# Hybrid attention block on one core: scores made once in two-bank tiles, probabilities scaled and transposed by TensorE, sinks' blocks first, output projection beside blocks

## Chip, cores and metric

One Trainium2 chip; the kernel runs on one of its cores. The metric is the device time of the core in microseconds, the median of the runs shown. All inputs are 32-bit floats.

## The reference

Two layers over 1024 tokens of width 1024. Layer 0 is a mixer of two attentions, layer 1 an mLSTM; each is followed by a SwiGLU FFN with 2816 hidden columns. The change is in layer 0's mixer:

```python
qa, kc, vc, ks, vs, kw, vw, g, qb, kb, vb = split(h @ w_in)         # 2072 columns; 8 query heads on 2 key heads, 64 wide
# attention a, per block of 128 queries, for three sets of keys:
#   compressed (63 keys), selected (16 of 16 key blocks: all earlier ones), window (512)
p = masked_softmax(q @ k.T * scale, mask);  o_i = p @ v
o_a = gate_0 * o_c + gate_1 * o_s + gate_2 * o_w                     # gates = sigmoid(g + gate_bias)
# attention b, per block: window of 128, and a sink in the softmax
mx = max(logits.max(-1), sink);  e = exp(logits - mx)
o_b = (e / (e.sum(-1) + exp(sink - mx))) @ v
h = h + concat(o_a, o_b) @ w_out
```

## The kernel before

All products are made in the type F32R from split operands: a value x is hi (its rounding, made by a copy) and lo = x - hi. `product` (line 138) makes one 128x512 output from k chunks with three matmuls each (hi x hi, hi x lo, lo x hi): 24 for the input projection, 12 for the output projection here. `split_w` (line 122) makes the parts of weights; `load_w` brings them with one DMA.

Queries are written to DRAM (`qs`) and read back per block with head dimension on partitions. K and V stay in SBUF pages. `page(tag)` takes pages from five pools with a fixed count each (`PAGES`); PSUM tiles come from `acc` and `tmp_ps` and, for the statistics, from a third tag "ts".

A block is 128 queries of one key head g: four heads r, so 512 columns. There are 16 blocks of attention a ("NSA blocks", kind 0) and 16 of attention b ("sinks' blocks", kind 1). `block` (line 523) is a generator of four steps:

1. three DMAs bring the queries as qa and qb (line 531), GpSimd clears the rest of qb (line 533).
2. `scores_stats` (line 488): for each head r the scores with queries on partitions (two matmuls per stretch of keys, lines 496 and 498), the row's minimum of negated masked scores (line 507; line 503 without mask) and the exponent with its sum (line 509). Only minimum and sum are kept.
3. the correction (minimum, log of sum, log of gate, per query and key set) is joined, split, transposed by TensorE (line 612) and written into qb's lower rows (line 613).
4. for each chunk of 128 keys the scores are made again with keys on partitions: matmuls of qa (line 639), qb with the correction (line 640) and, on masked chunks, of the mask (line 642); the exponent (line 644) is then the final probability, split by `parts` (lines 103, 105, 108), and goes into two value products (lines 646 and 647). At the end `po` is copied (line 649), its two halves are joined and split by GpSimd (lines 101, 653, 654) and written to DRAM (`os`).

`blocks` (line 665) keeps four blocks in flight, each one step behind the next. `mixer_ab` (line 676) runs the first part of the input projection alone (compressed keys, first half of qa, selected and window keys and values, gates). Then it draws one dense product per block: the 16 of the second part (rest of qa, attention b's columns) beside the 16 NSA blocks, then the output projection of attention a (`ab_out(0)`, line 694) beside the sinks' blocks. The output projection of attention b, with the next norm, follows at the end.

The order in which each engine runs its instructions is set when the program is built: a planner takes what it expects to be ready, earlier written work first, so that dense products fill gaps of the blocks and the other way round. At run time each engine keeps that order.

## Time and profile before

| what | value |
|---|---|
| median of 3 runs | 2661.21 us (2660.42 to 2661.75) |
| profiled execution | 2661.99 us, its span 2660.3 us |
| mean granted TensorE clock | 0.987 |
| TensorE busy | 2578.3 us (97%) |
| VectorE, ScalarE, GpSimd busy | 1344.4, 725.5, 480.4 us |

Busy times are of one profiled execution. A matmul's row shows its whole passage (about 0.39 us for 512 columns) while the next one starts much earlier, so counts in a stretch say more than durations. Clock 1.00 is 2.4 GHz, the lower level 1.2 GHz; a number between is a mean over a stretch.

### The profile page before, as it was taken

The page shows a single profiled execution, that of the slowest core. Times are in us where ns is not written, and L with a number is a line of the kernel's source. Part 1 is how long each engine was busy: PE and PEld are TensorE (multiplying, and loading weights), DVE is VectorE, ACT ScalarE, POOL GpSimd, SP SyncE. Part 2 cuts the span into 40 slices and gives each one's busy share as a digit, 9 for nine tenths or more (in the row PEclk, how much of TensorE's full clock was granted, in tenths as well). Part 3 has the DMA queues.
Part 4 walks back from the last instruction along what each step waited for, and adds up shares of the span by engine and source line. Part 5 has one row for each costly group of instructions (what it writes and reads, how often), then busy time and mean ns, then how long its engine had stood idle before and what let it go on. Part 6 is the DMA issues. An engine that isn't in the chain of part 4 may idle for free.

```text
span 2660.3 us, 29873 instructions
## 1 busy us (share of the span) xinstructions
PE 2578.3 (97%) x11365; PEld 2053.8 (77%) x11365; DVE 1344.4 (51%) x2675; ACT 725.5 (27%) x1685; POOL 480.4 (18%) x542
## 2 busy tenths in 40 slices
PE   8999999988999999999999999999999999999998
PEld 6877777665778888888887777788788888888886
DVE  4368878988643333333336554545533333333335
ACT  4247768744210000000002343332210000000013
POOL 3322132154301010101012111112110101010102
PEclk9999999989999999999999999999999999999999
DMA  6222131343311111111113111112111111111112
GB/s 192 89 71 72 51 97 28 112 108 83 102 48 48 48 48 48 48 48 48 48 48 112 52 41 40 36 56 95 48 32 55 41 50 46 48 48 48 56 48 79
DMA packets 178899, 167.36 MB, mean 63 GB/s; under 512 B 15220, under 2 KB 156740, under 8 KB 178756
## 3 DMA queue, kind: packets, MB, share of 16 engines
q1 hardware_dynamic: 178756, 165.46, 20.1%
q8 instruction: 89, 1.46, 0.2%
q14 instruction: 54, 0.44, 0.0%
HBM read 136.02 MB, written 29.38 MB: 62 GB/s over the span
## 4 chain that ended last, share of the span: by engine, by line
PE 86%; DVE 7%; ACT 2%; issue 2%; POOL 1%; DMA 1%; SPq 0%; DVEq 0%; ACTq 0%; POOLq 0%
PE acc L144 12%; PE acc L145 12%; PE acc L143 12%; PE pg L145 6%; PE pu L144 6%; PE pu L143 6%; PE pu L145 6%; PE pg L144 6%; PE pg L143 6%; PE po L647 2%; PE po L646 2%; DVE lo L108 1%; PE sps L498 1%; PE sps L496 1%; PE st L639 1%
## 5 line engine op out<-in xcount | busy, mean ns | idle before, releaser
L103 ACT CAST whl<-ws 128x1024 fp32r<-128x1024 f32 (+2 forms) x112 | 95.0, 848 | 870.1 <-PE acc L145 435.2
L144 PE MATMUL acc<-lo,whl 128*128 128x512 f32 x800 | 316.2, 395 | 0.0
L143 PE MATMUL acc<-hi,whl 128*128 128x512 f32 x800 | 315.2, 394 | 0.0
L145 PE MATMUL acc<-hi,whl 128*128 128x512 f32 x800 | 314.1, 393 | 0.0
L101 POOL TENSOR_SCALAR whl<-ws 128x1024 fp32r<-128x1024 f32 (+2 forms) x132 | 116.0, 879 | 1011.7 <-PE acc L145 472.0
L143 PE MATMUL pu<-xh,whl 128*128 128x512 f32 x704 | 279.7, 397 | 0.0
L145 PE MATMUL pg<-xh,whl 128*128 128x512 f32 x704 | 278.2, 395 | 0.6 <-DVE whl L108 0.6
L143 PE MATMUL pg<-xh,whl 128*128 128x512 f32 x704 | 278.1, 395 | 0.0
L145 PE MATMUL pu<-xh,whl 128*128 128x512 f32 x704 | 278.1, 395 | 0.0
L144 PE MATMUL pu<-xl,whl 128*128 128x512 f32 x704 | 278.1, 395 | 0.0
L144 PE MATMUL pg<-xl,whl 128*128 128x512 f32 x704 | 278.0, 395 | 0.0
L143 PE MATMUL acc<-xh,whl 128*128 128x512 f32 x640 | 262.8, 411 | 0.1
L144 PE MATMUL acc<-xl,whl 128*128 128x512 f32 x640 | 259.2, 405 | 2.5 <-DVE xl L200 2.3
L145 PE MATMUL acc<-xh,whl 128*128 128x512 f32 x640 | 257.4, 403 | 0.5 <-DVE whl L108 0.5
L108 DVE TENSOR_TENSOR whl<-ws,whl 128x1024 fp32r<-128x1024 f32 (+2 forms) x222 | 220.1, 991 | 39.5 <-ACT whl L103 23.0
L238 DVE TENSOR_TENSOR u<-pu,rb 128x512 f32<-128x512 f32 x88 | 60.8, 691 | 353.9 <-PE pu L145 353.9
L788 DVE TENSOR_TENSOR h<-h,acc 128x512 f32<-128x512 f32 x176 | 120.7, 686 | 231.8 <-PE acc L145 231.7
L143 PEld LDWEIGHTS acc<-hi,whl 128*128 128x128 f32 x800 | 150.3, 188 | 36.3 <-POOL hi L101 0.3
L145 PEld LDWEIGHTS acc<-hi,whl 128*128 128x128 f32 x800 | 150.2, 188 | 35.4
L144 PEld LDWEIGHTS acc<-lo,whl 128*128 128x128 f32 x800 | 150.1, 188 | 34.8 <-DVE lo L108 0.2
L766 ACT ACTIVATE g<-g 128x512 f32<-128x512 f32 x88 | 55.5, 631 | 437.6 <-DVE g L238 436.8
L101 POOL TENSOR_SCALAR hi<-u 128x512 fp32r<-128x512 f32 x88 | 82.8, 941 | 486.4 <-DVE u L769 486.4
(316 smaller groups left out, 4563.1 us busy)
## 6 DMA issues: line engine op xcount, KB each, us to landing
ws<-in_ffn_w_gate SPq DMA_DIRECT2D x22, 1024.0 KB
ws<-in_ffn_w_up SPq DMA_DIRECT2D x22, 1024.0 KB
ws<-in_ffn_w_down SPq DMA_DIRECT2D x40, 512.0 KB
spill<-h SPq DMA_DIRECT2D x32, 256.0 KB
qa<-qs SPq DMA_DIRECT2D x64, 128.0 KB
os<-o SPq DMA_DIRECT2D x64, 128.0 KB
h<-spill SPq DMA_DIRECT2D x32, 256.0 KB
oh<-os SPq DMA_DIRECT2D x32, 256.0 KB
```

Source lines behind the costliest of these rows:

```text
L101: nc.gpsimd.tensor_scalar(out, in_, 1.0, 0.0, op0=OP.mult, op1=OP.add)
L103: nc.scalar.copy(out, in_)
L108: self.nc.vector.tensor_tensor(out, in_, hi.bitcast(F32), op=OP.subtract)
L143: nc.tensor.matmul(ps, w[:, 0, k], xh, start=(start and k == 0), stop=False)
L144: nc.tensor.matmul(ps, w[:, 0, k], xl, start=False, stop=False)
L145: nc.tensor.matmul(ps, w[:, 1, k], xh, start=False, stop=(stop and k == n - 1))
L238: nc.vector.tensor_tensor(out, ps, self.rb(hf), op=OP.mult)
L496: nc.tensor.matmul(p[:, at:at + n], qa[:, r * P:(r + 1) * P], ka, start=True, stop=False, skip_group_check=True)
L646: nc.tensor.matmul(po, vt, eh, start=(i == 0), stop=False)
L647: nc.tensor.matmul(po, vt, el, start=False, stop=(i == len(todo) - 1))
L766: silu = nc.scalar.activation(g, g, AF.Silu)
L788: nc.vector.tensor_add(h, h, ps)
```

## The change

Scores are made once. `scores` makes them with queries on partitions in a tile S of two PSUM banks (two of them), 1024 columns wide, so that one row of any key set fits; a stretch of keys that crosses the border between the banks is cut. One masked minimum and one exponent per head follow, the exponent written to SBUF (page "x"; "w" for compressed keys and sinks' blocks). `weights` makes one factor per row (from sum and gate, or sum and sink) and GpSimd scales the four rows. `values` transposes 128x128 pieces of the scaled probabilities with TensorE, four into one bank T, ScalarE copies hi, VectorE subtracts lo, and two value products follow per chunk. `blocks` writes, for each unit (a block's key set): weights of the unit before, scores of this unit, values of the unit before. Queries are loaded two blocks ahead with four DMAs.

K pages hold hi and lo in their two halves (one page instead of two). The gate is kept as 1 + exp(-z). During the mixer `acc` and `tmp_ps` have two tiles each. A pair of hi and lo in tag "x" is one page of double width; the count of "x" pages goes from 32 to 16.

Attention b's columns come first in the input projection (`first`, 12 products), then its blocks run beside the rest (`second`, 20 products and the gates, 22 steps drawn over 15 blocks). The NSA blocks run beside the output projection of attention b (`out1`, 16 products, two per block in the first eight) and beside half of that of attention a (`out0`, 8 products, one per block from n = 4 on). The other half (8 products) follows with the norm of both halves. h is kept in "k" pages and layer 0's hid in "h" pages. The core of the diff:

```diff
-PAGES = {"x": 32, "h": 16, "k": 20, "w": 10, "q": 8}
+PAGES = {"x": 16, "h": 16, "k": 20, "w": 10, "q": 8}
...
+    def pair(self, tag, name):
+        if tag == "x":
+            t = self.page("x", name, F32R, w=2 * H5)
+            return t[:, :H5], t[:, H5:]
+        return self.page(tag, name, F32R), self.page(tag, name, F32R)
     def acc(self, name="acc"):
+        if self.attn:
+            return self.ps.tile([P, H5], F32, name=name, tag="pa", bufs=2)
         return self.ps.tile([P, H5], F32, name=name, tag="acc", bufs=3)
     def tmp_ps(self, name="tp"):
+        if self.attn:
+            return self.ps.tile([P, H5], F32, name=name, tag="T", bufs=2)
         return self.ps.tile([P, H5], F32, name=name, tag="tp", bufs=3)
...
-        xh = self.page("x", f"xh", F32R)
-        xl = self.page("x", f"xl", F32R)
+        xh, xl = self.pair("x", "xh")
...
+            k = self.page("h" if br < 2 else "k", "K", F32R)
+            s, o = slice(64 * g, 64 * g + 64), slice(64 - 64 * g, 128 - 64 * g)
+            self.hi_copy(k[s], kf[s], "act")
+            self.lo_sub(k[o], kf[s], k[s])
+            self.K[br, g, hf] = k
...
-                nc.vector.tensor_scalar(z, z, self.gbias, None, op0=OP.add)
-                self.log_sigmoid(z, z)
...
+                nc.vector.tensor_scalar(z, z, self.gbias, -1.0, op0=OP.add, op1=OP.mult)
+                nc.vector.tensor_scalar(z, z, 88.0, None, op0=OP.min)
+                nc.scalar.activation(z, z, AF.Exp)
...
+        first = [(KB, [k_tile(2), v_tile(2)]), (QB, [q_tile(1, 0), q_tile(1, 1)]),
+                 (QB + 256, [q_tile(1, 2), q_tile(1, 3)])]
+        second = [(KC, [c_tile(0), c_tile(1)]), (KS, [k_tile(0), v_tile(0)]), (KW, [k_tile(1), v_tile(1)]),
+                  (QA, [q_tile(0, 0), q_tile(0, 1)]), (QA + 256, [q_tile(0, 2), q_tile(0, 3)])]
         first, second = [[part(*x) for x in xs] for xs in (first, second)]
+        return chain(*first), chain(*second, g_part())
...
+                k = self.at.tile([P, 64], F32R, name=f"kc{g}")
+                nc.vector.memset(k.bitcast(F32), 0.0)
+                nc.scalar.copy(k[0:64, :nb], po[:64, :nb])
+                nc.vector.tensor_tensor(k[64:128, :nb], po[:64, :nb], k[0:64, :nb].bitcast(F32), op=OP.subtract)
+                self.Kc[g] = k
...
-    def scores_stats(self, qa, qb, parts, width, mask, nm, ls):
...
+    def load_q(self, kind, g, n):
+        nc = self.nc
+        qa, qb = self.pair("q", "qa")
+        for i, t in enumerate((qa, qb)):
+            src = self.qs[kind, i, 256 * g:256 * g + 256, n * P:(n + 1) * P].rearrange("(r d) q -> d r q", d=64)
+            for k in range(2):
+                self.last_q = nc.sync.dma_start(t[64 * k:64 * k + 64].bitcast(F32).rearrange("d (r q) -> d r q", r=4), src)
+        return qa, qb
...
+    def units(self, kind, g, n):
+        def vals(br, first):
+            return [self.V[br, g, j // 4][:, (j % 4) * P:(j % 4 + 1) * P] for j in range(first, n + 1)]
+        mks, mkw = (m.rearrange("p a b -> p (a b)") for m in (self.mks, self.mkw))
         if kind == 0:
+            first = max(0, n - 4)
+            w, ww = (n + 1) * P, (n + 1 - first) * P
+            return [(0, [(self.Kc[g], 0)], 64, self.mkc[:, 56 - 8 * n:120 - 8 * n], [self.Vc[g]]),
+                    (1, self.key_parts(0, g, 0, n), w, mks[:, 1024 - w:], vals(0, 0)),
+                    (2, self.key_parts(1, g, first, n), ww, mkw if n >= 4 else mks[:, 1024 - ww:], vals(1, first))]
+        first = max(0, n - 1)
+        w = (n + 1 - first) * P
+        return [(3, self.key_parts(2, g, first, n), w, self.mkw[:, 0:5:4] if n else self.mkw[:, 4], vals(2, first))]
...
+    def scores(self, q, unit, g):
+        nc = self.nc
+        br, parts, w, mask, _ = unit
+        qa, qb = q
+        st = self.sm.tile([P, 4, 4], F32, name="st", bufs=6)
+        es = []
+        if br == 0:
+            ec = self.page("w", "ec", w=256).rearrange("p (r k) -> p r k", r=4)
+        for r in range(4):
+            h = slice(r * P, (r + 1) * P)
+            p = self.ps.tile([P, 2 * H5], F32, name="S", bufs=2)
+            cuts = []
+            for k, at in parts:
+                n = k.shape[1]
+                m = min(n, H5 - at % H5)
+                cuts.append((k[:, :m], at))
+                if m < n:
+                    cuts.append((k[:, m:], at + m))
+            for k, at in cuts:
+                n = k.shape[1]
+                for i, qq in enumerate((qa, qb)):
+                    nc.tensor.matmul(p[:, at:at + n], qq[:, h], k, start=i == 0, stop=i == 1, skip_group_check=True)
+            s = p[:, :w]
+            sv = s.rearrange("p (a b) -> p a b", a=mask.shape[1]) if len(mask.shape) == 3 else s
+            nm, l = st[:, 0, r:r + 1], st[:, 1, r:r + 1]
+            nc.vector.tensor_tensor_reduce(sv, sv, mask, -1.0, 1e20, OP.add, OP.min, nm)
+            if br == 3:
+                nc.vector.tensor_tensor(nm, nm, self.sink[:, 4 * g + r:4 * g + r + 1], op=OP.min)
+            if br == 0:
+                e = ec[:, r]
+            elif br == 3:
+                if r % 2 == 0:
+                    e2 = self.page("w", "e3")
+                e = e2[:, r % 2 * 256:r % 2 * 256 + w]
             else:
+                e = self.page("x", "e", w=w)
+            nc.scalar.activation(e, s, AF.Exp, bias=nm, scale=-1.0, accum_out=l)
+            es.append(e)
+        return st, es
...
+    def weights(self, unit, g, n, st, es):
+        nc = self.nc
+        br = unit[0]
+        nm, l, t, f = (st[:, i] for i in range(4))
+        if br == 3:
+            nc.vector.tensor_tensor(t, nm, self.sink[:, 4 * g:4 * g + 4], op=OP.subtract)
+            nc.scalar.activation(t, t, AF.Exp)
+            nc.vector.tensor_tensor(t, t, l, op=OP.add)
         else:
+            ig = self.ig[:, n, g * 12:(g + 1) * 12].rearrange("p (r b) -> p b r", b=3)[:, br]
+            nc.vector.scalar_tensor_tensor(t, l, 0.5, ig, op0=OP.max, op1=OP.mult)
+        nc.vector.reciprocal(f, t)
+        for r in range(4):
+            nc.gpsimd.tensor_scalar(es[r], es[r], f[:, r:r + 1], 0.0, op0=OP.mult, op1=OP.add)
+    def values(self, unit, es, po, first, last):
+        nc = self.nc
+        br, _, w, _, vals = unit
+        for j, v in enumerate(vals):
+            tp = self.tmp_ps("T")
+            n = min(P, w)
+            for r in range(4):
+                nc.tensor.transpose(tp[:n, r * P:(r + 1) * P], es[r][:, j * P:j * P + n], self.ident)
+            eh, el = self.pair("k", "eh")
+            if br == 0:
+                for t in (eh, el):
+                    nc.gpsimd.memset(t[64:128].bitcast(F32), 0.0)
+            nc.scalar.copy(eh[:n], tp[:n])
+            nc.vector.tensor_tensor(el[:n], tp[:n], eh[:n].bitcast(F32), op=OP.subtract)
+            nc.tensor.matmul(po, v, eh, start=first and j == 0, stop=False)
+            nc.tensor.matmul(po, v, el, start=False, stop=last and j == len(vals) - 1)
...
-    def block(self, kind, g, n, big):
...
+        work = []
+        for b in todo:
+            us = self.units(*b)
+            work += [(b, u, i == 0, i == len(us) - 1) for i, u in enumerate(us)]
+        qs = {}
+        def ahead(i):
+            if i < len(todo):
+                qs[todo[i]] = self.load_q(*todo[i])
+        ahead(0)
+        ahead(1)
+        done = None
+        for i in range(len(work) + 1):
+            cur = work[i] if i < len(work) else None
+            prev = done
+            if prev:
+                self.weights(prev[0][1], prev[0][0][1], prev[0][0][2], *prev[1])
+            if cur:
+                (kind, g, n), unit, first, last = cur
+                if first:
+                    ahead(todo.index(cur[0]) + 2)
+                done = (cur, self.scores(qs[cur[0]], unit, g))
+            if prev:
+                b, unit, first, last = prev[0]
+                if first:
+                    po = self.acc("po")
+                self.values(unit, prev[1][1], po, first, last)
+                if last:
+                    self.outputs(*b, po)
+                yield b, last
...
+            self.h = [[None] * NC for _ in range(2)]
+            n = 0
+            for i, _ in enumerate(self.blocks([(1, g, n, ) for n in range(8) for g in range(2)])):
+                want = (i + 1) * 22 // 15
+                while n < want and next(second, self) is not self:
+                    n += 1
+            for _ in second:
                 pass
+            out1 = self.ab_out(1, (0, 1))
+            out0 = self.ab_out(0, (0,))
+            for b, last in self.blocks([(0, g, n) for n in range(8) for g in range(2)]):
+                if last and next(out1, self) is self and b[2] >= 4:
+                    next(out0, None)
+                elif last:
+                    next(out1, None)
+            for _ in chain(out1, out0):
+                pass
+        self.attn = False
         self.norm_begin()
+        for c, _ in enumerate(self.ab_out(0, (1,))):
+            for hf in range(2):
+                self.norm_chunk(self.h[hf][c], hf, c, "nf", 0)
...
+    def ab_out(self, part, hfs):
         nc = self.nc
         w_out = self.a["ab_w_out"][0]
+        xs = {hf: [] for hf in hfs}
+        for hf in hfs:
             for c in range(4 * part, 4 * part + 4):
+                t = self.page("x", "oh", F32R, w=2 * H5)
+                with self.behind():
+                    nc.sync.dma_start(t.bitcast(F32).rearrange("p (i t) -> p i t", i=2),
+                                      self.os[:, c * P:(c + 1) * P, hf * H5:(hf + 1) * H5].rearrange("i p t -> p i t"))
+                xs[hf].append((t[:, :H5], t[:, H5:]))
         for c2 in range(4):
             ws = self.load_w(w_out[H5 * part:H5 * part + H5, c2 * 256:(c2 + 1) * 256], 4)
+            for i in range(2):
+                c = c2 * 2 + i
+                w = self.split_w(ws[i])
+                for hf in hfs:
+                    if part:
+                        h = self.h[hf][c] = self.page("k", "h")
+                        with self.behind():
+                            nc.sync.dma_start(h, self.spill[c][:, hf * H5:(hf + 1) * H5])
                     h = self.h[hf][c]
                     ps = self.acc()
                     self.product(ps, w, xs[hf])
                     nc.vector.tensor_add(h, h, ps)
                     yield
+    def behind(self):
+        return self.tc.issue_after(self.last_q.ins)
...
-                        hid[m + i, hf] = self.parts(u, "k", "pool")
+                        hid[m + i, hf] = self.parts(u, "k" if last else "h", "pool")
```

## Rows read from the trace of the kernel before

**Rows 1.** The page's first part: busy time of an engine, its share of the span, its instructions.
```profile
PE 2578.3 (97%) x11365; PEld 2053.8 (77%) x11365; DVE 1344.4 (51%) x2675; ACT 725.5 (27%) x1685; POOL 480.4 (18%) x542
```

**Rows 2.** Busy time by stretch: from:to and length in us, busy us and instructions of TensorE, its weight loads, VectorE, ScalarE and GpSimd, granted clock, DMA share, GB/s.
```profile
20.00:50.00 30.00, 25.15 (x138) 18.36 (x139) 20.08 (x39) 13.65 (x31) 10.86 (x11) 1.00 0.62 194
50.00:100.00 50.00, 50.00 (x294) 41.32 (x294) 10.61 (x19) 7.50 (x16) 11.03 (x8) 0.90 0.32 107
100.00:175.00 75.00, 71.86 (x326) 56.06 (x325) 36.17 (x76) 21.29 (x58) 25.49 (x21) 0.95 0.24 72
175.00:500.00 325.00, 307.85 (x1398) 243.60 (x1397) 276.35 (x849) 244.31 (x731) 77.41 (x74) 0.97 0.23 70
500.00:650.00 150.00, 128.16 (x543) 96.06 (x542) 131.46 (x340) 82.00 (x232) 70.22 (x74) 0.93 0.36 96
650.00:723.00 73.00, 65.44 (x257) 49.05 (x258) 47.58 (x70) 17.53 (x29) 26.40 (x28) 0.95 0.35 110
800.00:1460.00 660.00, 660.00 (x2837) 531.50 (x2835) 256.35 (x344) 66.31 (x95) 84.01 (x105) 1.00 0.17 54
```

**Rows 3.** The chain of work that ended last, 655 to 725 us: start, duration, what.
```profile
662.31 0.59 ACT oc L649
...
667.57 3.92 DMA os<-o
671.50 4.91 DMA oh<-os
...
717.32 0.51 PE pg L145
```

**Rows 4.** Waits, 175 to 735 us: engine and line, for whom it waited, us in total, times, longest.
```profile
ACT sps L509 <- DVE st L507: 30.8, 47, 3.3
...
PE po L647 <- DVE lo L108: 15.8, 20, 1.5
```

**Rows 5.** TensorE in order of time (start, duration, what), in five places: score matmuls of 256, of 64 and of 384 columns, matmuls of 512 columns where the clock had fallen (with the row of busy time by stretch for it), and the transposes of h (with theirs).
```profile
343.77 0.28 PE L496 MATMUL sps<-ka,qa 128*128 128x256 f32 x1
343.89 0.28 PE L498 MATMUL sps<-kb,qb 88*128 88x256 f32 x1
...
362.12 0.28 PE L496 MATMUL sps<-kac,qa 128*128 128x64 f32 x1
362.23 0.28 PE L498 MATMUL sps<-kbc,qb 88*128 88x64 f32 x1
...
368.91 0.34 PE L496 MATMUL sps<-ka,qa 128*128 128x384 f32 x1
369.09 0.34 PE L498 MATMUL sps<-kb,qb 88*128 88x384 f32 x1
...
585.86 0.63 PE L143 MATMUL acc<-oh,whl 128*128 128x512 f32 x1
586.29 0.63 PE L144 MATMUL acc<-oh,whl 128*128 128x512 f32 x1
...
2575.77 7.15 PE L804 MATMUL tp<-ident,h 128*128 128x128 f32 x64
...
580.00:590.00 10.00, 9.79 (x34) 8.04 (x35) 7.75 (x23) 3.65 (x14) 3.75 (x4) 0.66 0.32 80
...
2576.00:2582.60 6.60, 6.60 (x63) 6.60 (x62) 1.88 (x2) 6.14 (x13) 1.06 (x1) 1.00 0.01 2
```

**Rows 6.** Groups of TensorE instructions, 40 to 735 us: line, operation, tiles, count, busy us and mean ns of one, idle before.
```profile
L496 PE MATMUL sps<-ka,qa 128*128 128x256 f32 (+3 forms) x264 | 85.0, 330 | 1.8 <-ACT sps L509 1.0 <-DVE h L719 0.4 <-DMA qa<-qs 0.4
...
L647 PE MATMUL po<-lo,vt 128*128 128x512 f32 x162 | 72.3, 446 | 8.9 <-DVE lo L108 8.8
...
L639 PE MATMUL st<-qa,ka 128*128 128x512 f32 x162 | 68.0, 419 | 2.7 <-ACT e L644 1.7 <-DVE qf L240 0.5 <-DVE qb L613 0.4
...
L642 PE MATMUL st<-identr,mk 128*128 128x512 f32 x70 | 28.6, 409 | 0.0
...
L464 PE MATMUL tp<-kvs,cw 128*64 128x63 f32 x128 | 15.6, 296 | 0.0
L496 PE MATMUL sps<-kac,qa 128*128 128x64 f32 x64 | 14.3, 240 | 0.9 <-ACT sps L509 0.9
```

**Rows 7.** VectorE in order of time (start, duration, what), then groups (as above) of VectorE and ScalarE, 40 to 735 us, and of GpSimd, whole span.
```profile
474.21 0.69 DVE L503 TENSOR_REDUCE st<-sps 128x1 f32<-128x512 f32 x1
474.81 0.69 DVE L507 CUSTOM_DVE_ANT_0 sps<-sps,mk 128x512 f32<-128x512 f32 x1
475.42 0.14 DVE L507 DVE_READ_ACCUMULATOR2_ANT st<- 128x1 f32 x1
475.42 0.69 DVE L108 TENSOR_TENSOR lo<-e,hi 128x512 fp32r<-128x512 f32 x1
...
L105 DVE CAST hi<-e 128x512 fp32r<-128x512 f32 x108 | 48.1, 445 | 0.7 <-ACT e L644 0.2
...
L509 ACT ACTIVATE sps<-sps,st 128x512 f32<-128x512 f32 x72 | 47.7, 662 | 14.4 <-DVE st L507 7.4 <-DVE st L503 6.5
...
L101 POOL TENSOR_SCALAR whl<-ws 128x1024 fp32r<-128x1024 f32 x76 | 81.4, 1071 | 615.0 <-PE acc L145 258.0 <-PE pu L145 201.0 <-issue 138.3
L199 POOL TENSOR_SCALAR xh<-h,vec 128x512 fp32r<-128x512 f32 x64 | 57.0, 894 | 136.7 <-DVE h L739 41.1 <-DVE h L719 28.8 <-DVE h L788 28.4
...
L101 POOL TENSOR_SCALAR whl<-ws 128x512 fp32r<-128x512 f32 x52 | 32.9, 633 | 373.8 <-PE acc L145 203.8 <-issue 168.9 <-POOL xh L199 0.5
```

More of the change, by code (lines that the diff above doesn't have):

```diff
@@ L648, in block, with outputs @@
+    def outputs(self, kind, g, n, po):
+        nc = self.nc
         c = self.page("w", "oc")
@@ L660, in blocks @@
     def blocks(self, todo):
-        live = [None] * 4
-        for b in list(todo) + [None] * 3:
-            live = [self.block(*b) if b else None] + live[:3]
-            for i in ORDER:
-                if live[i]:
-                    next(live[i], None)
-            yield
+        work = []
[27 more added lines that the diff above has]
+                yield b, last
     def mixer_ab(self):
```

242 lines of the change are left out of this document (25 added, 217 removed).

## The prediction

> **What bounds the kernel now.** I read the page's engine totals first: TensorE is busy 97% of the span and no other engine more than 51% [rows 1]. That makes it the suspect everywhere, but a modelled busy time is no rate, so I read the busy time by stretch next, beside the granted clock. In the first FFN (800 to 1460 us) TensorE is busy all the time at clock 1.00 and issues 2837 matmuls in 660 us, 0.233 us each [rows 2]: this is what a 128x512 matmul costs when nothing is late. The change touches nothing there. It touches 20 to 717 us, where layer 0's mixer runs; the first FFN product starts at 717.3 us [rows 3].
>
> Inside it the stretches differ. I multiply busy share by clock for a net share. 175 to 500 us (NSA blocks beside 24-matmul input products): 307.85/325 = 0.95, times 0.97, 0.92. 500 to 650 us (sinks' blocks beside 12-matmul output products): 128.16/150 = 0.85, times 0.93, 0.79. There VectorE is busy 131 of 150 us [rows 2]: TensorE waits for small VectorE steps. So the stage is TensorE's, with VectorE close behind (0.85 of 175 to 500 us), and it gets worse where the dense products beside the blocks get thin. PE waits named by the profile are short: 20 waits for the lo part before a value product, 15.8 us in all [rows 4].
>
> A second measure counts work. Priced at 0.233 us per 512-column matmul, at the issue distances of [rows 5] for smaller ones (0.12 us for 256 columns, 0.175 for 384, 0.11 for 64 and 128) and 0.11 us per transpose, the stage holds: input products 16x2x24 x 0.233 = 179; output products 8x2x2x12 x 0.233 = 90; transposed scores (162 + 16)x2 matmuls and 70 + 16 mask matmuls (the 16s are the compressed chunk, one per NSA block), 442 x 0.233 = 103; value products 356 x 0.233 = 83; statistics' scores, 264+64 pairs, 97 by their shapes in the code (72, 88, 40 and 128 pairs of 512, 256, 384 and at most 128 columns); compression, gates and transposes some 40 [rows 6]. Sum 592 us in 697: 0.85. Over 20 to 717 us busy times clock is about 0.88, so waits too short to show as idle take another 0.03.
>
> **The change part by part.** *Scores once.* Removed from TensorE: 356 transposed score matmuls (83 us), 86 mask matmuls (20 us), 32 transposes of the correction, one per block (3.5 us): 106.5 us. Added: four transposes for each of 178 key chunks, 712 x 0.11 = 78 us. The before's own 64 transposes of h in one go took 7.15 us at clock 1.00 [rows 5], 0.11 us each, and they are the same operation on the same shape. Rows of 640 columns and more are cut at the bank border: for n = 5, 6, 7 one more cut per row and query part, 48 small matmuls x 0.11 = 5 us. Net 23 us less on TensorE.
>
> *VectorE, ScalarE, GpSimd.* VectorE loses 108 copies of hi parts [rows 7], the write of the correction and some dozen small operations per block; it keeps one masked minimum per row (now up to 1024 columns) and one lo part per chunk. Consecutive 512-column operations start 0.60 us apart although each is shown as 0.69, and reading the accumulator costs no start [rows 7]: so 0.07 + 0.00104 us per column. For the NSA blocks: 71680 score columns in 192 rows, 88 us; 148 lo parts x 0.6 = 89; some 20 of small ones; 30 of dense work beside them: 227 us. ScalarE: exponents at 0.66 us for 512 columns [rows 7], copies at 0.59 [rows 3]: about 200 us. GpSimd gets new work, the scaling of probabilities: 1.05 us for 1024 columns in the nearest row (weights, 1071 ns), 0.89 for 512 by the dearer one (xh with a scale per partition) [rows 7]; so between 0.2 us a row + 0.00085 us a column (from that row and its 512-column sister, 633 ns) and 0.00175 us a column, 99 to 125 us for the NSA rows. I take the lower, because that row has the larger tile; with the unchanged outputs it stays well under 285 us. Against TensorE's sum below, none of the three is the bound. The scaling is cheap as work and dear as a wait: the four rows of a unit (up to 4 x 1.05 us) must all be done before the first transpose of that unit; behind a waiting transpose on TensorE stand the unit's value products and the dense and score matmuls that the planner put after them. What hides it is the next unit's scoring, which the new loop writes between the two; without that cover 48 units x 2 to 4 us would show, 100 to 190 us.
>
> *Sinks' blocks first.* They now run beside 20 input products of 24 matmuls instead of 16 output products of 12. Start and first part: products begin at 20 to 21 us; 12 x 24 x 0.233 = 67, 9 us of transposes and waits at the start (5 us idle in 20 to 50 us [rows 2]): 97 us. Second part: 20 x 5.6 = 112, gates 7.5, compression and transposes 20 (its 128 matmuls show 15.6 us [rows 6]), blocks 44 (30 chunks x 0.9 + 17 of scores): 184 us of work. I take a share of 0.90, that of 50 to 500 us by the work count (net 0.92 less some), not the 0.76 of 500 to 650 us: the dense work beside it is of the first kind. 204 us, to 301. Exponents and compression's silu now alternate, so some more table loads fall to ScalarE; it has the room.
>
> *Output projection beside NSA blocks.* NSA work: values and transposes 148 x (4 x 0.11 + 2 x 0.233) = 134, scores 84, and 24 output products x 12 x 0.233 = 67: 285 us. What is lost is cover: 24 products of 2.8 us instead of 16 of 5.6, and two-deep buffers everywhere (score tiles, transpose tiles, accumulators, and in the later blocks the pairs of hi and lo, as h takes 16 of 20 "k" pages). The blocks stand between the two stretches of [rows 2]: net 0.92 and 0.79, by work 0.03 lower, 0.89 and 0.76. VectorE's load (227 of 285) is nearer to the first, the thin cover to the second; I take 0.82: 347 us, to 648. Bounds 0.89 and 0.76: 320 and 375.
>
> *Tail.* Now: last oc at 662.3, its parts to DRAM, back as oh by 676.4, FFN at 717.3 [rows 3]: 14 us of wait and 41 for 16 products. After: the same wait, then 8 products (22 us) with the norm's VectorE work beside them, and 4 us because 16 "x" pages hold the norm's 16 pairs only once the 4 of oh are free: 40 us, to 688. The loads of queries grow from 3 to 4 DMAs a block on SP, issued two blocks ahead, and the loads of oh and h are put behind them; each is needed a block later, so no time. Pages that change tags (hid in "h" with 16 instead of 20) are free again before the next group's first product is drained (11 us of matmuls): nothing. If that cover failed, a group would wait some 2 us, six times.
>
> *Sum.* 97 + 204 + 347 + 40 = 688 against 717: 29 to 30 us less. The profiled execution took 2662.0 us (span 2660.3); 2662 - 30 = 2632, and the median of the runs is 0.8 us under it: **2631 us**. The 30 us are 23 of TensorE work, some 20 for sinks' blocks under better cover, less some 13 given back in the NSA blocks.
>
> **A rule against it.** The clock first by rows: in the 6.6 us in which the before runs 63 transposes and nothing else the granted clock is 1.00 [rows 5]; in 50 to 100 us, with compression's narrow matmuls and TensorE never idle, it is 0.90 [rows 2]. The Trainium skill (TensorE: Matmul & The Clock Gate, Part 4: PE-mode transpose) says that transposes don't count as TensorE activity in the way matmuls do, and the full clock isn't granted for them. By that rule blocks rich in transposes would fall to 1.2 GHz and the sum would be near the third rival's; by the row they stay at 2.4 GHz and the sum stands.
>
> **The rivals.**
> 1. *Cover is as good as before.* The planner already mixes dense and block matmuls finely, and three other engines get lighter. NSA at 0.89 to 0.90: 318 us, **2602 us**. For it: VectorE falls from 0.85 to 227/318 = 0.71. Against: fewer dense products and shallower buffers.
> 2. *Two-deep loops in series (slower).* A score tile lives through its matmuls, the masked minimum and the exponent; with two tiles, half of the sum per row: 197 us for 192 rows from the durations above, 255 with 0.3 us of queueing at the two hand-overs. A transpose tile lives through 0.44 + 0.6 + 0.7 us and hand-overs: 148 us for 148 chunks, 192 with queueing. Side by side they hide under TensorE's 347; in series they are 447. It decides from 376 us on, that is, from 30% in series. At half, 397 us: **2683 us**. For it: even now 47 exponents waited 30.8 us for the minimum [rows 4], and the "x" pages leave room for only two units while the first output part holds 8. Against: values of one unit and scores of the next need different tiles and are both ready.
> 3. *Transposes lower the clock (slower).* Matmuls of 512 columns start 0.43 us apart where the clock has fallen to its lower level, 1.2 GHz [rows 5]. If the 296 NSA value products run so, they cost 296 x 0.20 = 59 us more: **2690 us**. Against: the 6.6 us of transposes at 1.00.
> 4. *No change.* The 23 us go into the new wait for the scaling and the stage ends where it did: **2661 us**.
>
> **How the numbers follow.** Forecast 0.42, rival 1 0.22, rival 2 0.23, rival 3 0.05, rival 4 0.08. Within 0.2% (5.3 us), about what a measurement of this kernel tells from no change: 0.08. Faster 0.42 + 0.22 = 0.64; slower 0.23 + 0.05 = 0.28. The forecast's own range is 2608 to 2650. The 8-in-10 range reaches over rival 1 and most of rival 2, NSA 320 to 400 us and 10 us for the other stages: 2594 to 2695.
>
> **What would show it.** Right: PE rows without 512-column st and mask matmuls, 712 transposes near 0.11 us; the sinks' blocks' stretch busy above 0.9 at a clock above 0.95; the NSA stretch some 350 us, VectorE under 0.75 there; the first FFN product at about 688 us; FFN and layer 1 as before. Wrong: idle TensorE before transposes released by GpSimd (the scaling isn't hidden), before score matmuls released by ScalarE (two score tiles are too few), or a clock well below 0.9 in the NSA stretch at high busy share; or VectorE above 0.85, which would mean that its new wide rows cost more than 0.00104 us per column.

## The result and the profile after

The changed kernel takes 2693.47 us (median of 4 runs, 2692.54 to 2694.53), the kernel before 2661.06; the ratio is 1.0122, 95% interval 1.0104 to 1.0139. It is 1.2% slower. The forecast said 2631; the time lies at the upper end of the range of 2594 to 2695. The profiled execution has a span of 2691.3 us.

The page's engine totals, to be read beside [rows 1]:

```profile
PE 2553.3 (95%) x11651; PEld 2058.7 (76%) x11651; DVE 1255.7 (47%) x2416; ACT 675.2 (25%) x1448; POOL 563.4 (21%) x750
```

TensorE is busy for 25 us less, but that is no sign of less work in the mixer: behind the first FFN product it is busy 1889.23 us instead of 1923.80, and ahead of it 653.80 of 761 us (from 20 us on) instead of 642.78 of 697. The clock there is 0.92 for 0.96, so busy time times clock, a rough measure of work, is 601 us for 617: some 16 us less, at a net share of 0.79 for 0.89. Busy time by stretch (columns as in [rows 2]):

```profile
20.00:781.00 761.00, 653.80 (x3212) 503.45 (x3211) 428.05 (x1124) 333.21 (x859) 299.67 (x432) 0.92 0.31 90
100.00:330.00 230.00, 200.53 (x1029) 161.96 (x1027) 111.24 (x347) 81.55 (x230) 82.24 (x110) 0.90 0.38 104
330.00:380.00 50.00, 35.73 (x127) 24.36 (x127) 18.04 (x73) 14.60 (x53) 18.34 (x36) 0.66 0.40 125
380.00:730.00 350.00, 319.19 (x1655) 240.22 (x1654) 233.41 (x610) 200.87 (x510) 165.84 (x255) 0.98 0.22 60
730.00:781.00 51.00, 27.06 (x86) 20.30 (x86) 27.57 (x38) 11.28 (x19) 20.82 (x21) 0.73 0.26 78
800.00:1460.00 660.00, 660.00 (x2901) 544.16 (x2900) 251.73 (x336) 65.02 (x90) 73.86 (x83) 1.00 0.15 48
```

The first score of a sinks' block starts at 99.67 us, the first of an NSA block at 328.79; the last sinks' oc is copied at 351.74, the last oc of all at 729.91, and the first FFN product starts at 780.59, where it was 717.32 [rows 3]. So the mixer ends 63.3 us later. From there to the end it takes 2691.3 - 780.6 = 1910.7 us, where it was 2660.3 - 717.3 = 1943.0: 32.3 us are won back in code that the change does not touch. The last line shows how: 2901 TensorE instructions in the 660 us of the FFN that held 2837 before [rows 2], 0.2275 us each for 0.2326, with TensorE always busy at clock 1.00 in both. The last oc and the first FFN product (start, duration, what, idle time before and its releaser):

```profile
729.91 0.59 ACT L604 COPY oc<-po 128x512 f32<-128x512 f32 x1 [1.31 <-PE po L599]
780.59 0.39 PE L155 MATMUL pg<-xh,whl 128*128 128x512 f32 x1
```

What the blocks wait for is seen best in order of time. TensorE first (start, duration, what, idle time before and its releaser), then GpSimd, in the same 10 us of the NSA blocks:

```profile
565.13 1.01 PE L545 MATMUL S<-K,qa 128*128 128x384 f32 x6
567.22 0.33 PE L591 MATMUL T<-ident,e 128*128 128x128 f32 x1 [1.08 <-POOL e L581]
568.10 0.33 PE L591 MATMUL T<-ident,e 128*128 128x128 f32 x1 [0.55 <-POOL e L581]
568.98 0.44 PE L591 MATMUL T<-ident,e 128*128 128x128 f32 x2 [0.55 <-POOL e L581]
...
570.00 0.62 PE L591 MATMUL T<-ident,e 128*128 128x128 f32 x4
...
572.52 0.27 PE L591 MATMUL T<-ident,e 128*128 128x128 f32 x1
```

```profile
562.84 0.61 POOL L113 TENSOR_SCALAR o<-oc 64x512 fp32r<-64x512 f32 x1 [2.43 <-ACT oc L604]
563.53 1.28 POOL L608 TENSOR_TENSOR ot<-oc,o 64x512 f32<-64x512 f32 x1
564.89 1.27 POOL L609 TENSOR_TENSOR o<-oc,ot 64x512 fp32r<-64x512 f32 x1
566.26 3.55 POOL L581 TENSOR_SCALAR e<-e,st 128x768 f32<-128x768 f32 x4
```

The four rows of a unit are scaled one after the other, 3.55 us for 768 columns, and only after the outputs of the block before, which hold GpSimd from 562.84 to 566.16. Each first transpose comes just behind its row's scaling: for 3 us TensorE runs at GpSimd's pace, and the scores behind the first of these transposes start only at 569.17. In all, from 95 to 735 us (for whom it waited, us in total, times, longest):

```profile
PE T L591 <- POOL e L581: 25.0, 36, 3.0
```

### The profile page after: what moved, and what is told of

Same layout as the page of the kernel before. It is cut to its first block, busy times and chain, and to the rows that moved or that the text cites. A ratio compares the mean times of both kernels' runs of the same rounds, so it can differ in the third digit from the quotient of the medians.

```text
span 2691.3 us, 30365 instructions
## 1 busy us (share of the span) xinstructions
PE 2553.3 (95%) x11651; PEld 2058.7 (76%) x11651; DVE 1255.7 (47%) x2416; ACT 675.2 (25%) x1448; POOL 563.4 (21%) x750
## 4 chain that ended last, share of the span: by engine, by line
PE 77%; POOL 5%; DVE 5%; issue 3%; ACT 2%; DMA 1%; SPq 0%; POOLq 0%; DVEq 0%; ACTq 0%
PE acc L157 10%; PE acc L155 10%; PE acc L156 10%; PE pu L157 6%; PE pu L156 6%; PE pu L155 6%; PE pg L155 6%; PE pg L157 6%; PE pg L156 6%; POOL e L581 2%; PE T L591 2%; PE S L545 2%; PE po L598 2%; PE po L599 1%; POOL xh L210 1%
## 5 line engine op out<-in xcount | busy, mean ns | idle before, releaser
L115 ACT CAST whl<-ws 128x1024 fp32r<-128x1024 f32 (+2 forms) x127 | 107.5, 846 | 897.0 <-PE acc L157 480.0
L155 PE MATMUL acc<-hi,whl 128*128 128x512 f32 x800 | 315.1, 394 | 0.0
L157 PE MATMUL acc<-hi,whl 128*128 128x512 f32 x800 | 314.5, 393 | 0.0
L156 PE MATMUL acc<-hi,whl 128*128 128x512 f32 x800 | 314.0, 393 | 0.0
L113 POOL TENSOR_SCALAR whl<-ws 128x1024 fp32r<-128x1024 f32 (+2 forms) x125 | 109.9, 879 | 966.5 <-PE acc L157 422.2
L155 PE MATMUL pu<-xh,whl 128*128 128x512 f32 x704 | 275.6, 391 | 0.0
L157 PE MATMUL pu<-xh,whl 128*128 128x512 f32 x704 | 274.1, 389 | 1.4 <-DVE whl L120 1.4
L157 PE MATMUL pg<-xh,whl 128*128 128x512 f32 x704 | 274.2, 389 | 0.2 <-DVE whl L120 0.2
L155 PE MATMUL pg<-xh,whl 128*128 128x512 f32 x704 | 274.3, 390 | 0.0
L156 PE MATMUL pg<-xh,whl 128*128 128x512 f32 x704 | 274.0, 389 | 0.0
L156 PE MATMUL pu<-xh,whl 128*128 128x512 f32 x704 | 273.9, 389 | 0.0
L120 DVE TENSOR_TENSOR whl<-ws,whl 128x1024 fp32r<-128x1024 f32 (+2 forms) x252 | 246.9, 980 | 43.8 <-ACT whl L115 24.8
L155 PE MATMUL acc<-xh,whl 128*128 128x512 f32 x640 | 259.6, 406 | 1.2 <-POOL xh L210 1.2
L156 PE MATMUL acc<-xh,whl 128*128 128x512 f32 x640 | 254.9, 398 | 1.3 <-DVE xh L211 1.0
L157 PE MATMUL acc<-xh,whl 128*128 128x512 f32 x640 | 254.0, 397 | 0.0
L157 PEld LDWEIGHTS acc<-hi,whl 128*128 128x128 f32 x800 | 150.1, 188 | 35.0
L156 PEld LDWEIGHTS acc<-hi,whl 128*128 128x128 f32 x800 | 150.2, 188 | 34.7 <-DVE hi L120 0.2
L155 PEld LDWEIGHTS acc<-hi,whl 128*128 128x128 f32 x800 | 150.4, 188 | 33.8 <-POOL hi L113 0.3
```

What stands on the lines that cost most here:

```text
L113: nc.gpsimd.tensor_scalar(out, in_, 1.0, 0.0, op0=OP.mult, op1=OP.add)
L115: nc.scalar.copy(out, in_)
L120: self.nc.vector.tensor_tensor(out, in_, hi.bitcast(F32), op=OP.subtract)
L155: nc.tensor.matmul(ps, w[:, 0, k], xh, start=(start and k == 0), stop=False)
L156: nc.tensor.matmul(ps, w[:, 0, k], xl, start=False, stop=False)
L157: nc.tensor.matmul(ps, w[:, 1, k], xh, start=False, stop=(stop and k == n - 1))
```

## The experiments

**The part that became faster.** The x pages now hold hi and lo side by side. The first kernel brings only this into the kernel before (h, k and all attention as before):

```diff
-PAGES = {"x": 32, "h": 16, ...
+PAGES = {"x": 16, "h": 16, ...
-        xh = self.page("x", f"xh", F32R)
-        xl = self.page("x", f"xl", F32R)
+        xh, xl = self.pair("x", "xh")     # one page of 1024 columns; also ka/kb, vt, oh in "x"
```

> The kernel before with one thing of the change: pages of tag x are of double width and hold hi and lo side by side. Theory P (the change's FFN and input products start 0.227 us apart instead of 0.233 because hi and lo share one page): all matmuls on x pages get 0.0066 us shorter, 4224 in the two FFNs, 768 in layer 0's input and 1150 in layer 1's, 40 us less in all: 2615 to 2630 us, and the first FFN shows about 2900 matmuls in 660 us instead of 2837. Rival (the spacing comes from something else in the change, such as h in k pages and hid in h pages): 2661 us within 3, 2837 matmuls in 660 us.

2622.54 us, ratio 0.9858 (0.9844 to 0.9873): the gain comes with the pages, not with the attention. But a pair also lies elsewhere. The place of a page is fixed when the program is built: as bytes past a multiple of 256 on each partition, the split weights (whl) start at 128 in all kernels but the last one here; x and h pages start at 160 in the kernel before; x pages at 128 in e1 and in the changed kernel. Two runs took place and pairing apart:

```diff
 # e9, in the kernel before
-PAGE = 516
+PAGE = 528
 # e10, in the changed kernel
-        t = self.pg.tile([P, 2 * H5 if tag == "x" else H5 if tag == "h" else PAGE], ...)
-        return t[:, :w]
+        at = 8 if tag in "xh" else 0
+        t = self.pg.tile([P, 2 * H5 + 16 if tag == "x" else H5 + 16 if tag == "h" else PAGE], ...)
+        return t[:, at:at + w]
```

> The kernel before with only the width of its k, w and q pages changed, from 516 to 528 words. Nothing is paired; but every page, the x and h pages behind them too, then starts at a multiple of 64 bytes on its partition, where in the kernel before the x and h pages start 32 bytes past one (in the changed kernel, and for x pages in e1, they start at a multiple). Theory A (it is the start of the moving operand that sets 0.227 or 0.233 us a matmul, and the pairing in e1 only moved it): products start 0.227 us apart, and since the h pages move too, 2605 to 2625. Theory P (hi and lo in one page): no change, 2655 to 2665.

> The changed kernel with x and h pages 16 words wider and used from word 8 on, so that they start 32 bytes past a multiple of 64, hi and lo still in one x page. Theory A: products in the FFN start 0.233 us apart again, 2725 to 2745. Theory P: as the changed kernel, 2688 to 2698.

e10: 2730.50, ratio 1.0266 (1.0250 to 1.0281): pairs alone give nothing. e9: 2635.55, ratio 0.9908 (0.9893 to 0.9922): no pairs, and two thirds of e1's gain. Theory P fell, and theory A had its size wrong. The same edit with 544 words instead of 528 put x and h pages at 0:

> The kernel before with k, w and q pages of 544 words instead of 516 and nothing else, so that these pages and the x and h pages behind them start at a multiple of 128 bytes (before: x and h at 32 past a multiple of 64; e9: an odd multiple of 64; x in e1 and in the changed kernel: a multiple of 128). Theory A in steps (0.233 us at 32, 0.229 to 0.231 at an odd multiple of 64, 0.227 at a multiple of 128): FFN products 0.227 us apart and layer 1's products on h pages, 0.231 to 0.233 in all runs so far, 0.227 too; median 2605 to 2618. Theory P with A (start at 64 is enough, the rest of e1's gain is from the pairing): as e9, 2631 to 2639.

2652.37, ratio 0.9973 (0.9961 to 0.9984): both readings in that expectation were wrong; a finer start is not a faster one. What was left is the place relative to the weights' 128. The same edit with 576 words puts all pages at 128; its counterpart moves the pairs of the changed kernel to 0 (32 words of offset instead of e10's 8, x pages only):

> The kernel before with k, w and q pages of 576 words instead of 516 and nothing else. All pages, x and h among them, then start 128 bytes past a multiple of 256, as the split weights do in every kernel so far and as the x pages of e1 and of the changed kernel do; in e13 x and h started at multiples of 256 (and kept 0.234 and 0.230 us), in e9 at 192 past one, in the kernel before at 160. Theory B (the place within 256 bytes sets it: the closer to the weights' own 128, the faster): products on x pages 0.226 to 0.228 us apart without any pairing, those on h pages 0.228 to 0.230, median 2612 to 2626. Theory P with a place (hi and lo must also be neighbours in one page): x products stay at 0.230 or more, 2632 to 2655.

> The changed kernel with x pages 64 words wider and used from word 32 on: still pairs of hi and lo in one page, still at a multiple of 128 bytes, but at a multiple of 256 instead of 128 past one. Theory B: products on x pages 0.233 or 0.234 us apart, 2718 to 2740. Theory P (paired, and at a multiple of 64 or 128): 2688 to 2700.

2610.96, ratio 0.9808 (0.9793 to 0.9822), and 2723.75, ratio 1.0234 (1.0217 to 1.0251), e17 as theory B had it, e16 just below its range. Last, e16 with the weights moved to 0 and all else left:

```diff
-        w = self.wp.tile([P, 2, 8, P], F32R, name="whl", tag="whl")
+        w = self.wp.tile([P, 2112], F32R, name="whl", tag="whl")[:, 32:2080].rearrange(...)
```

> e16 with the split weights' tiles 64 words wider and used from word 32 on, so that the weights start at multiples of 256 bytes while x, h, k, w and q pages stay 128 past one. Theory B in its relative form (what counts is the distance between the moving operand's place and the weights' place within 256 bytes): products 0.233 us apart again, 2650 to 2672. Theory B in its absolute form (the moving operand's own place counts): as e16, 2607 to 2616.

2657.55, ratio 0.9988 (0.9978 to 0.9998): nearly all of e16's gain is gone although no x or h page changed its place within 256 bytes. Moving either operand alone takes the gain away, so neither operand's own place sets it. What is left is the distance between them, or a need that both lie at 128; these runs don't tell the two apart. Busy time of the FFN's stretch in e16, e17 and e18:

```profile
800.00:1460.00 660.00, 659.62 (x2904) 544.96 (x2904) 269.65 (x364) 75.46 (x104) 87.93 (x110) 1.00 0.18 56
```

```profile
800.00:1460.00 660.00, 660.00 (x2853) 536.30 (x2852) 248.28 (x331) 63.73 (x88) 73.16 (x82) 1.00 0.15 48
```

```profile
800.00:1460.00 660.00, 660.00 (x2839) 534.49 (x2838) 259.37 (x347) 66.96 (x96) 85.58 (x106) 1.00 0.17 55
```

| kernel | x page, weights (bytes past 256) | distance | TensorE instructions in 660 us |
|---|---|---|---|
| before | 160, 128 | 32 | 2837 |
| e9 | 192, 128 | 64 | 2868 |
| e13 | 0, 128 | 128 | 2843 |
| e16 | 128, 128 | 0 | 2904 |
| e18 | 128, 0 | 128 | 2839 |
| e1 (h at 160) | 128, 128 | 0 | 2886 |
| changed | 128, 128 | 0 | 2901 |
| e10 | 32 or 96 away | 32, 96 | 2827 |
| e17 | 0, 128 | 128 | 2853 |

About a third of these instructions belong to the FFN's second product, which reads hid pages at other places, so the counts mix distances. Taken by operand from the starts in the same stretch, matmuls on x pages are on average 0.227 us apart in e1, e16 and the changed kernel (distance 0), 0.229 in e9 (64), 0.232 in e17 and e18 and 0.233 in e13 (128), 0.233 in the kernel before and in e10 (32 and 96); on the changed kernel's hid pages, at 192 and so 64 away, 0.229. A shorter distance is not always the faster one: 64 is better than 32.

**The wait for the scaling.** Theory Q: the mixer is late because transposes wait for probabilities to be scaled. e4 leaves the scaling out, and with it the division by the sum, the gates and the sinks' share:

```diff
-        for r in range(4):
-            nc.gpsimd.tensor_scalar(es[r], es[r], f[:, r:r + 1], 0.0, op0=OP.mult, op1=OP.add)
```

> The changed kernel without the scaling of the probabilities on GpSimd (left out: the division by the sum, the gate and the sink's part; the factors are still made). Theory Q: the scaling is what TensorE waits for, in both stretches; 48 NSA units and 16 blocks give 1 to 2 us each: 2615 to 2650 us. Rival (buffers of two tiles and the dense cover set the pace): 2675 to 2693 us, with the waits named for GpSimd now named for ScalarE's exponent or copy.

2646.55, ratio 0.9949 (0.9935 to 0.9964): 47 us less. The first FFN product starts at 733.87 instead of 780.59. Its stretches, cut at the same events as those of the changed kernel:

```profile
100.00:317.00 217.00, 194.10 (x1023) 159.34 (x1023) 105.29 (x346) 81.13 (x230) 50.64 (x49) 0.91 0.40 108
317.00:367.00 50.00, 37.99 (x139) 26.36 (x138) 19.50 (x78) 15.53 (x56) 11.89 (x15) 0.66 0.46 138
367.00:685.00 318.00, 303.38 (x1650) 234.84 (x1648) 228.62 (x607) 197.13 (x506) 63.48 (x80) 0.99 0.23 66
685.00:734.00 49.00, 25.53 (x85) 19.26 (x86) 27.18 (x38) 10.98 (x19) 20.51 (x21) 0.72 0.27 81
```

The NSA stretch loses 32 us (350 to 318, with as many TensorE instructions, 1650 for 1655), the sinks' stretch 13 (230 to 217); the 50 us between them and the tail stay. Is it order, queue or engine? e8 moves only the order: values are written two units behind the scores, the scaling still one behind. (In the sinks' stretch each dense product is then drawn one step earlier.)

```diff
-        done = None
-        for i in range(len(work) + 1):
+        done = []
+        for i in range(len(work) + 2):
...
+            prev = done.pop(0) if i >= 2 else None
...
-                done = (cur, self.scores(qs[cur[0]], unit, g))
+                done.append((cur, self.scores(qs[cur[0]], unit, g)))
```

> The changed kernel with the loop over units taken one step further apart: a unit's probabilities are scaled one unit after its scores as before, but transposed and multiplied by values two units after, so the scaling has the scoring of one more unit to hide behind. Theory Q (the wait is one of order, and cover hides it): 20 to 40 us of the 47 come back, median 2653 to 2675. Rival (GpSimd's throughput, or too few pages for three units in flight: the x pages hold 16 rows): no gain or a loss, 2690 to 2715.

2663.04, ratio 1.0013 (1.0004 to 1.0023): 30 us come back with not one instruction fewer. The last sinks' oc comes at 342.92 instead of 351.74 and the last oc of all at 696.32 instead of 729.91: 9 us are won before the first of the two, 25 between them. Busy time among the NSA blocks, with busy share (0.955) and clock as without scaling:

```profile
380.00:695.00 315.00, 300.94 (x1632) 234.19 (x1630) 227.33 (x592) 196.26 (x496) 163.97 (x248) 0.99 0.23 65
```

The queue (e3: the outputs' hi on ScalarE, ot and o on VectorE) and the engine (e6: the scaling on VectorE):

```diff
 # e3
-        self.hi_copy(o[0:64], c[0:64], "pool")
+        self.hi_copy(o[0:64], c[0:64], "act")
-        nc.gpsimd.tensor_tensor(t[64:128], ...); nc.gpsimd.tensor_tensor(o[64:128], ...)
+        nc.vector.tensor_tensor(t[64:128], ...); nc.vector.tensor_tensor(o[64:128], ...)
 # e6
-            nc.gpsimd.tensor_scalar(es[r], ...)
+            nc.vector.tensor_scalar(es[r], ...)
```

> The changed kernel with a block's output steps on ScalarE (hi) and VectorE (ot, o) instead of GpSimd, so that GpSimd's queue holds the scaling alone. Theory Q (a unit's scaling stands behind the outputs of the block before, 2.6 to 3.2 us a block, and TensorE has nothing to run meanwhile): 16 sinks' blocks give 2 to 3 us each and 16 NSA blocks 1 each, 35 to 60 us less: 2635 to 2660 us. Rival (two accumulator tiles are what leaves TensorE without a dense product; GpSimd's steps only end the same wait): 2680 to 2693 us.

> The changed kernel with the scaling of probabilities (L581) on VectorE instead of GpSimd. Theory Q by latency and queue (a scaling stands 0.5 to 1.1 us on GpSimd, behind outputs of 1.29 us): VectorE has the room (about half of 50 to 730 us) and does it faster, so most of the 47 us that leaving the scaling out gave comes back: median 2650 to 2668. Rival (VectorE is the next bound, its queue holds masked minima and lo parts, so that the scaling waits there as long): median 2680 to 2705, and transposes wait for DVE at L581 instead of POOL.

e3: 2682.28, ratio 1.0084 (1.0069 to 1.0099), 11 us, in the rival's range and not in theory Q's. They are won in the sinks' stretch: its last oc comes at 338.99, as early as without scaling (338.34), while the NSA blocks take no less than before. In the first stretch, then, taking the outputs out of GpSimd's queue does as much as leaving the scaling out; among the NSA blocks it does nothing, and more cover does. e6: 2685.70, ratio 1.0101 (1.0086 to 1.0116), 8 us only, in the rival's range too, though not with its sign: transposes wait only 5.3 us for VectorE's scaling, while value products wait 11.5 us for ScalarE's hi, for 8.1 in the changed kernel. VectorE scales 640 columns in 584 ns where GpSimd takes 812, but in the NSA stretch its queue is fuller: 290.39 us busy in 342, 0.85, against 233.41/350 = 0.67.

```profile
380.00:722.00 342.00, 316.19 (x1649) 236.21 (x1647) 290.39 (x778) 196.03 (x508) 64.06 (x78) 1.00 0.21 61
```

**What else could be late.** e2 draws the gates early (`chain(second[0], g_part(), *second[1:])`); e5 gives the sinks' stretch one-bank score tiles and three accumulators and transpose tiles; e7 has 14 "w" pages instead of 10; e12 is e8 with the NSA blocks n = 3, 2, 1, 0 before 4 to 7.

> The changed kernel with the gates' part of the input projection drawn after the compressed keys' part instead of last. Theory G (330 to 352 us is the gates' chain alone, with no block and no product beside it): 10 to 18 us less than the changed kernel, 2675 to 2684 us, and TensorE above 0.8 busy up to the first NSA block. Rival (the stretch waits for the last sinks' blocks and not for the gates; the wait only moves): 2690 to 2695 us.

> The changed kernel with its PSUM laid out otherwise while the sinks' blocks run: score tiles of one bank (they hold 256 columns there), and three accumulators and three transpose tiles instead of two of each; the NSA blocks keep their layout. Theory Q (the sinks' stretch is 50 us late because transposes wait for the scaling of probabilities on GpSimd): depth of the other tiles changes little, the first NSA score stays at 344 to 351 us and the median at 2685 to 2694. Rival (two-deep tiles in series: accumulators and transpose tiles): the stretch shortens by 20 us or more, median 2660 to 2675.

> The changed kernel with 14 pages of tag w instead of 10 (they hold the sinks' probabilities, the gates and the outputs). Theory Q: pages are not what waits, median 2688 to 2695. Rival (the page shortage holds back exponents and outputs in the sinks' stretch, where issue gaps of 4 to 5 us stand on the chain at 283 and 312 us): 5 to 15 us less, 2678 to 2688.

> As e8, with the NSA blocks of the first half in the order n = 3, 2, 1, 0 instead of 0, 1, 2, 3. Theory H (at the hand-over, 310 to 370 us, the short blocks n = 0 and 1 have too little work for TensorE while the last sinks' outputs travel to DRAM and back before the first output product can start; clock 0.50 to 0.76 there): longer blocks fill it, 8 to 15 us less than e8, 2648 to 2655. Rival (the hand-over is the gates' and the last outputs' latency, whatever block stands behind): within 4 us of e8, 2659 to 2667.

e2: 2688.34, ratio 1.0106 (1.0089 to 1.0123), 5 us, between its two readings. e5: 2687.38, 1.0109 (1.0094 to 1.0124), 6 us: its first NSA score comes 42 us earlier (287.16), yet its last sinks' oc only 6 (345.32) and its last oc 1 (728.82). Here deeper tiles moved scores forward and hardly shortened the chain. e7: 2693.95, nothing, as theory Q had it. e12: 2667.78 against e8's 2663.04: theory H fell. Most of the hand-over between the two kinds of blocks is thus unexplained by any one of gates, pages or block length. The chain there (start, duration, what):

```profile
335.72 0.62 PE tp L406 x4
336.33 0.62 PE tp L178
336.95 0.43 PE tp L179
...
351.74 0.57 ACT oc L604
352.41 0.62 POOL o L113
353.11 1.27 POOL ot L608
354.44 1.27 POOL o L609
...
366.82 8.86 DMA oh<-os
375.72 0.50 PE acc L155
```

The gates' narrow product runs alone; the last part of the sinks' outputs reaches an output product only at 375.72; and 512-column matmuls start 0.43 us apart, as where the clock has fallen in [rows 5]. TensorE is idle for 14.3 of the 50 us (330 to 380), some 10 of them before the transposes of the gates; drawing the gates early still won only 5.

**Put together.** e11 is e8, e2 and e3 in one; e14 and e15 are the changed kernel and e11 with pages of 544 words, so that x and h pages stand at 128 as in e16.

> The changed kernel with values two units behind (e8), gates drawn early (e2) and the outputs' parts on ScalarE and VectorE (e3) together. Theory Q (one wait behind GpSimd's queue, gates apart from it): e8 has 30 of the 47 us that leaving the scaling out gave; the outputs give some 6 more and the gates 5, median 2648 to 2656, still above the kernel before with aligned pages by 30 or more, because the hand-over between the two kinds of blocks stays. Rival (the three are independent and add: 30 + 5 + 11): 2645 to 2648 or less.

> The changed kernel with pages of 544 words, so that its k, w, q and h pages start at multiples of 128 bytes as its x pages already do. It compares the two kernels at equal starts: theory A gives some 10 to 20 us on h and k pages (layer 1's products, value products), 2672 to 2684, and against the kernel before at 128 a loss of 55 to 75 us: the change in its own parts. Theory P: 2690 to 2697.

> e11 (values two units behind, gates early, outputs off GpSimd) with pages of 544 words. Theory: what e14 gains on the changed kernel it gains here too, 2622 to 2634, and it stays 10 to 20 us above the kernel before at 128. Rival (with cover, scores made once pay): at or below the kernel before at 128.

e11: 2642.72, ratio 0.9936 (0.9920 to 0.9953): 51 us less than the changed kernel, 5 more than the three apart add up to, so the rival's reading is the nearer. e14: 2687.63, 1.0105 (1.0090 to 1.0120), between its two ranges. e15: 2636.05, 0.9911 (0.9896 to 0.9925), slower than its range. Against e16's 2610.96 the change costs 77 us at nearly equal places, and 25 with its waits covered (5% of the matmuls on split weights are still 128 apart in e14 and e15, an estimated 3 us at the spacings above). e16, the kernel before with wider pages, is the fastest of all that ran.

## Why the prediction was wrong

The sum said 688 us for the first FFN product; it is 780.6, 93 late. The prediction left FFN and layer 1 as before; they gave back 32. 93 - 32 is the 62 us between 2631 and 2693.

**The step that failed** is "What hides it is the next unit's scoring". The price was right (2 to 4 us a unit, and four rows of 768 columns took 3.55 us), and so was the place, though a transpose waits only for its own row and not for all four; the cover was taken for granted. Its sign is the one that the prediction had named: idle TensorE before transposes, released by GpSimd. The next unit's scoring does stand between scores and transposes, but GpSimd can't begin before the reciprocal (from 95 to 735 us it sat idle 95.3 us, in 30 waits for one), and in the sinks' stretch it also stands behind outputs of 1.3 us each (e3), so the scoring is over first. It cost 47 of the 93 us (e4), of which one more unit of cover returns 30 (e8). The waits that the profile names show less: 25.0 us of idle TensorE before transposes of e.

**Terms by stage**, each from the event of the line above to its own (us):

| until | forecast | changed | e3 | e4 | e8 | e11 |
|---|---|---|---|---|---|---|
| first sinks' score | 97 | 99.7 | 100.1 | 99.5 | 99.5 | 100.4 |
| last sinks' oc | 204 | 252.1 | 238.9 | 238.9 | 243.4 | 231.0 |
| last oc | 347 | 378.2 | 381.5 | 346.3 | 353.4 | 346.3 |
| first FFN product | 40 | 50.7 | 48.6 | 49.3 | 50.6 | 49.7 |

NSA blocks: 31 us over the forecast, and the scaling is all of it: without it, or with its waits covered (e11), they take the forecast's 347. (The share of 0.82 was picked between two bounds; that it fits to 1 us is partly luck.) Sinks' stretch: 48 us over, 13 of them the scaling. The share of 0.90 did not come: 100 to 330 us has a net share of 0.87 x 0.90 = 0.78, that of the old sinks' stretch, and 0.81 without scaling; the thick input products did not lift it, and why is open. Gates and hand-over had no term at all. Tail: 11 us over. Its 14 us of wait showed as 11.7 us of idle TensorE, but the 8 products then took 39 us, not 26. They ran partly at the lower clock (0.73 in the tail), and 12.4 us of idle time stood between them, most of it for lo parts of the split weights, which VectorE made behind the norm's steps. The two longest waits there:

```profile
PE acc L155 <- DMA oh<-os: 11.7, 1, 11.7
PE acc L157 <- DVE whl L120: 9.5, 2, 5.3
```

**Steps that held.** 712 transposes start (0.62 - 0.27)/3 = 0.12 us apart for 0.11 by [rows 5]; TensorE's work in the mixer falls by some 16 us (busy time times clock, a rough measure) for 23 forecast; VectorE's load in the NSA stretch is 0.67, under the 0.75 named; the loads of queries show one wait of 0.7 us; more "w" pages gain nothing (e7).

**The rivals.** Rival 1's 318 us among the NSA blocks are not reached even with the waits covered (346.3 in e11). Rivals 3 and 2 gave 2690 and 2683 and lie nearest, but by other mechanisms. Rival 2 had tiles in series. TensorE waited 6.0 us for exponents before scores in 330 to 735 us, and e8 brings the stretch to 315 us with the same tiles. Three tiles for the NSA blocks were not tried. Rival 3 is not borne out: 380 to 730 us, where most transposes are, has clock 0.98. The Trainium skill (TensorE: Matmul & The Clock Gate, Part 4: PE-mode transpose) says that the full clock is not granted for transposes; this trace, at 0.98 with transposes among matmuls, does not show it. The clock is low where TensorE idles: 0.66 in the hand-over, where it was busy 35.73 of 50 us, 0.73 in the tail, 27.06 of 51.

**"As before"** for untouched code failed too, by 32 us: the change of page width moved the x pages from 160 to 128 within 256 bytes, and h pages from 160 to 192. That is shown by e10, e16, e17 and e18; the pairing itself gives nothing that these runs can tell.

**Open:** the 25 us that e15 still loses to e16. With e15's first FFN product at 730.97 and e16's at 711.70, 19 of them lie ahead of the FFN. There the sinks' stretch with the hand-over (clock 0.67 from 310 to 360 us in e15) and the tail are the weak ones, in e11 27 and 10 us over the forecast; no run took them away.

## What to carry to other kernels

A new step between two TensorE operations of a unit needs its whole latency covered, its place in the other engine's queue included; count that against the work written between, and put one more unit in between before moving the step to another engine. A change of any tile's size moves the places of all tiles behind it: compare kernels at equal places, or a gain of 1 or 2% is credited to the wrong edit. And a stage boundary added to a kernel (here sinks' blocks to NSA blocks) is a term of the sum, with its own idle time and its own low clock.

## What the runs showed of the hardware

Matmuls of 512 F32R columns on x pages, in an unbroken stream at clock 1.00 (800 to 1460 us), started 0.227 us apart where moving operand and weights lay at the same place within 256 bytes (e1, e16, the changed kernel), 0.229 where they lay 64 apart (e9), and 0.232 to 0.233 at 32, 96 or 128 apart (before, e10, e13, e17, e18). Over this kernel that is 50 us, 2%, for one constant. Why was not tested. In e13 and e17 the weights were at 128 and x at 0, in e18 the other way round, so neither place alone is enough. Whether the distance counts, or both have to be at 128, is not shown: both at 0 was not run.
